# A hybrid encoder's dilated attention stage: scores over the used keys, v's parts summed in PSUM, weights split over two steps

## The chip, the cores and the metric

One of the eight cores of a Trainium2 chip runs the whole kernel. The metric is the time in microseconds (us) of one execution on the chip. Engines are named as in the profile: PE is TensorE's matmuls and PEld its weight loads, DVE is VectorE, ACT is ScalarE, POOL is GpSimd, SP is SyncE. PSUM is the accumulator memory that PE writes.

## The reference

The reference is a two-layer encoder over 1024 tokens of width 1024. Layer 0 mixes tokens with multi-head latent attention. Layer 1, which the change touches, mixes them with dilated sliding-window attention: three groups with (window, dilation) of (128, 1), (512, 4) and (2048, 16), each with its own q, k and v of 16 heads of 64, merged by their softmax denominators. Each layer ends in a squared-ReLU MLP. Of a dilated group:

```python
half = window // (2 * dilation)          # 64 in all three groups
L = S // dilation                        # 1024, 256, 64 tokens of one residue
qr, kr, vr, pr = (_to_residues(t, dilation) for t in (q, k, v, pos))
...
valid = (ki >= 0) & (ki < L) & (abs(qi - ki) <= half)
s = einsum(q, k) + bias[t5_bucket(pk - pq)]      # only where valid
```

So after tokens are put in order of their residue, a query sees at most 64 neighbours on each side, and never past its residue. In group 2 a residue has 64 tokens, and a tile of 128 tokens holds two whole residues.

## The kernel before

The program first runs in half precision: each fp32 operand is written as two fp16 parts, high and low, and a product is three matmuls (high by high, low by high, high by low). An fp32 version follows that runs only if a range check fails; in the runs here it doesn't.

`dil` (line 2191) writes the dilated stage as a list of 96 steps `("qk", g, pr, tp)` and six empty ones: group g, head pair pr (two heads), and tp, a pair of token tiles of 128 tokens. A group is 32 steps, a pair four. One turn n of the loop holds work of several steps:

- `fetch_split(n + 1)`: if step n+1 is the first of a pair, the pair's q and k weights, two raw tiles `wqkr` of 128x1024, are written as high and low parts `wqk` (`parts`: ACT line 156 for the high part, DVE line 161 for the low one). `held` ties the ACT part to the ACT instruction before it in the program.
- `attend(ready)`: for two token tiles, `products` (scores `pss`, line 2345), `scores` (bias and maximum on DVE into `pd`, exponential on ACT), the parts `ph`, and one transposing DMA on SP's queue into `pT`.
- `fetch(n)`: loads of coming weights on SP's queue; `um`: for group 2, the outputs of the groups 0 and 1 of a head pair are fetched by issues on ACT's queue.
- `project` (48 matmuls in two halves, `psproj`): q and k of a step.
- `stacks`: between the two halves, the normalized q and k (`qn`) of the step before are transposed on PE (`psq`) and copied to `kT`, the high part by ACT (line 2321) and the low one by DVE (line 2322). The next turn's `products` read both.
- `av`: probabilities times v (`psav`, lines 2424 and 2425), for the tiles scored one turn before, then the sum over v's parts into `U` (line 2432).
- `qkstep`: the norm of q and k, ending in `qn` (line 2305).

At the end of a pair in group 2, `finish` merges the groups' outputs: small factors (`mgm`, `mgf`, `mgw`, `mgd`) on DVE with one exponential on ACT, then U times mgf (line 2506) on DVE, um times mgf on POOL, and two additions U+um (line 2508) on DVE for each half. `emit` transposes the result (`psot`).

PE's instructions run in the order of the program (`pin_from`). The order of the other engines is set by a scheduler that works from the program and its dependences, so the diff doesn't tell it.

For scores, `span(g, t)` gives the columns of the 256-key window that a tile reads afterwards; before, `products` computes all 256. For group 2, `span` is 64 to 192.

Of the kernel before, what the change touches and what calls it, by code (L numbers as in the profile page):

```python
# [20 lines left out]
P = 128  # L21
# [20 lines left out]
class K:  # L42
# [1915 lines left out]
    def dil_weights(self, g, pr, alloc=None, eng=None, parts=None):  # L1958


        w_in = self.a["dil_w_in"][0]
        raws = []

        def part(half, k):
            if k == 0:
                raws.append((alloc or self.G)("wqkr", (P, 4, 256), F32))
            c0 = (g * 3 + k) * 1024 + 2 * pr * 64
            (eng or self.nc.sync).dma_start(out=raws[half][:, :, k * P : (k + 1) * P],
                                            in_=w_in[half * 512 : (half + 1) * 512, c0 : c0 + P].rearrange("(d p) f -> p d f", p=P))

        for half in range(2):
            for k in range(2):
                if parts is None:
                    part(half, k)
                else:
                    parts.append(lambda half=half, k=k: part(half, k))

        def split():
            out = []
            for raw in raws:  # L1980
                hi, lo = self.pair(self.G, "wqk", (P, 4, 256))
                self.parts(hi, lo, raw, self.ws)
                out.append((hi, lo))
            return out

        return split
# [204 lines left out]
    def dil(self, at0, at1, tail, wqk, vd, back=None):  # L2191
# [138 lines left out]
        def span(g, t):  # L2330
            if g == 2:
                return 64, 192
            n = 8 if g == 0 else 2
            return 64 if t % n == 0 else 0, 192 if t % n == n - 1 else 256

        def window(g, t):
            return t // 2 * 256 if g == 2 else min(max(P * t - 64, 0), S - 256)

        def products(u, t, pss, i):
            w0 = window(u["g"], t)  # L2340
            q = u["q"].pop(t)
            for n, (a, b) in enumerate(((0, 0), (1, 0), (0, 1))):
                for e in range(2):
                    r = slice(64 * e, 64 * e + 64)
                    nc.tensor.matmul(pss[e][:, i * 256 : (i + 1) * 256], q[r, a, :], u["k"][r, b, w0 : w0 + 256],
                                     start=n == 0, stop=n == 2)

        def bias_load(u, t=0):
# [32 lines left out]
        def attend(pairs, pe):  # L2381
# [29 lines left out]
                nc.sync.dma_start_transpose(out=flat(pT).rearrange("p (b q) -> p b q", q=P), in_=flat(ph))  # L2411
            return [(u, t, parts(pT, i)) for i, (u, t) in enumerate(pairs)]

        def av(u, t, pT):
            g, pr = u["g"], u["pr"]
            n = 1 if g == 2 else 2
            ps = PS("psav")
            for e in range(2):
                for b in range(n):
                    v = u["V"][t + b][:, (2 * pr + e) % 4, :]  # L2420
                    if self.half:
                        o = ps[:, e * 128 : (e + 1) * 128]
                        c = slice((n * e + b) * P, (n * e + b + 1) * P)
                        nc.tensor.matmul(o, pT[:, 0, c], v, start=b == 0, stop=False)
                        nc.tensor.matmul(o[:, 0:64], pT[:, 1, c], v[:, 0:64], start=False, stop=b == n - 1)
                        continue
                    o = ps[:, e * 192 : (e + 1) * 192]
                    c = slice((n * e + b) * P, (n * e + b + 1) * P)
                    nc.tensor.matmul(o, pT[:, 0, c], v, start=b == 0, stop=False)
                    nc.tensor.matmul(o[:, 0:128], pT[:, 1, c], v[:, 0:128], start=False, stop=b == n - 1)  # L2430
            k = 2 if self.half else 3
            nc.vector.tensor_reduce(u["U"][:, t, :].rearrange("p (e d) -> p e d", e=2),
                                    ps[:, 0 : 128 * k].rearrange("p (e k d) -> p e d k", e=2, k=k), op=ALU.add, axis=AX.X)
            if t == 7:
                finish(u)
            elif t == 3 and (g, pr) == (2, 7):
                last(u, 0)
# [125 lines left out]
                f()  # L2563

        def fetch_split(n):
            if n in loads:
                self.held(lambda: wts.update({firsts[n][0:3]: loads.pop(n)()}))

# [57 lines left out]
        for n, step in enumerate(steps):  # L2626
            for f in vtodo.pop(n, ()):
                f()
            turn = step is not None and step[2:] == (0, 0) and bool(perms)
            if step is not None and step[1] < 2 and step[2] == 7 and step[3] >= 2:  # L2630
                if step[3] == 2:
                    new = [[[], []], [[], []]]
                    perms = [(step[1] + 1, dp, k) for dp in range(4) for k in range(2)]
                for _ in range(step[3] - 1):
                    permute(*perms.pop(0))
            w = None
            if step is not None:
                kind, g, pr, tp = step
                w = wts[(kind, g, pr)]
                if tp == 0:  # L2640
                    units[(g, pr)] = {"g": g, "pr": pr, "q": {}, "V": VSs[(g, pr // 2)],
                                      "k": D_("kT", (P, 2, S + 512), self.DT, 2), "U": self.G("U", (P, 8, P), F32)}
                u = units[(g, pr)]
            if self.half and step is not None and tp == 0:
                bias_load(u)
            fetch_split(n + 1)
            transposed, scored = scored, attend(ready, n > end) if ready else []
            fetch(n)
            for u_, t_, _ in scored:
                if u_["g"] == 2:  # L2650
                    if u_["pr"] < 7:
                        if t_ == 7:
                            um(u_, (0, 1))
                    elif t_ in (1, 5):
                        um(u_, (t_ // 4,))
            if turn:
                h = [(lambda k, d, t=t: t[k][d // 2][:, d % 2, :]) for t in new]
                ahead = [PS("psproj") for _ in range(2)]
                both(w, ahead, (0, 1))
                ps = ahead.pop(0)  # L2660
            elif step is not None and ahead:
                ps = ahead.pop(0)
            elif step is not None:
                ps = PS("psproj")
                project(h, w, ps, 0, 2 * tp)
                one = True
            ready, carry = carry, []
            stk.append(stacking)
            if len(stk) > 1:
                x = stk.pop(0)  # L2670
                if x is not None:
                    stacks(*x)
                    u_, tp_ = x[:2]
                    if u_["g"] == 2:
                        ready = ready + [(u_, 2 * tp_), (u_, 2 * tp_ + 1)]
                    else:
                        ready = ready + ([(u_, 2 * tp_ - 1), (u_, 2 * tp_)] if tp_ else [(u_, 0)])
                        carry = [(u_, 7)] if tp_ == 3 else []
            if turn:
                both(w, [ps] + ahead, (2, 3))  # L2680
                HT = new
            elif one:
                project(h, w, ps, 1, 2 * tp + 1)
            one = False
            if step is not None:
                if step[1:3] == (2, 7):
                    tail(tp)
            late, merged[:] = late + merged, []
            while late and (step is None or late[0][1] < n):
                u_, _, ths = late.pop(0)  # L2690
                emit(u_, ths)
            for x in transposed:
                x[0]["at"] = n
                av(*x)
            stacking = None
            if step is not None:
                stacking = (u, tp, qkstep(u, tp, ps))
                if n == end:
                    self.pin_from(mark, mybir.EngineType.PE)
                    banks.close()  # L2700
                    first = banks.enter_context(tc.tile_pool(name="psY", bufs=4, space=PSUM, reuse_waits="tile"))
                    psp[0] = ctx.enter_context(tc.tile_pool(name="psT", bufs=4, space=PSUM, reuse_waits="tile"))
                    if not self.half:
                        for pp in range(3):
                            self.reload(O, src, pp, 0, nc.sync)
            if self.half and n == end + 1:
                back()
                for pp in range(3):
                    self.reload(O, src, pp, 0, nc.sync)
# [197 lines left out]
```

## Time and profile before

| | before |
|---|---|
| median of 3 runs | 3000.55 us (2996.95 to 3000.91) |
| the profiled execution | 2996.41 us, span 2994.6 us |
| mean granted clock | 0.983 |
| PE, DVE, ACT, POOL busy | 2829.0, 2252.4, 1685.8, 922.5 us |
| dilated stage in the trace | about 1548.8 to 2303.5 us |

The rows of the profile give, for an instruction, its start, its duration in us, the engine, the line in the kernel, and what it writes and reads. In brackets stands how long the engine was idle before it and what ended that. In a table of groups, "busy, mean ns | idle before" is for all instructions of that form. In the table of waits, the columns are the total, how often, and the longest. PE's matmuls overlap one another, so that a row's duration is longer than the distance to the next start; the distance is what one costs.

### The profile page before, as it was taken

How to read it: one execution, taken by the hardware profiler on the slowest of the kernel's cores; microseconds unless marked ns; L12 is line 12 of the kernel's file. 1: busy time of each engine (PE TensorE's matmuls, PEld its weight loads, DVE VectorE, ACT ScalarE, POOL GpSimd, SP SyncE). 2: the span in 40 equal slices, each digit the busy share in tenths (PEclk: the TensorE clock that was granted, in tenths of full speed). 3: DMA queues.
4: the chain of work that ended last, by engine and by line, in shares of the span. 5: the costliest groups of instructions: out<-in, count | busy, mean ns of one | idle time of the engine just before them, and what ended most of it. 6: DMA issues, size and time to landing. Idle time of an engine off the chain costs nothing. (4 is left out here: it accounts for less than half of the span.)

```text
span 2994.6 us, 54486 instructions
## 1 busy us (share of the span) xinstructions
PE 2829.0 (94%) x20148; PEld 1679.2 (56%) x20148; DVE 2252.4 (75%) x4906; ACT 1685.8 (56%) x3491; POOL 922.5 (31%) x1272
## 2 busy tenths in 40 slices
PE   6878999999999999999999989988998999999998
PEld 5634566644444444444468878877875444444443
DVE  5687777658988866788768877777886699779565
ACT  4677888825455534543227777776664365555341
POOL 6578888700211000001123334454552001110010
PEclk9999999999999999999999999999998999999999
DMA  6267464325654799546536656665766455456753
GB/s 208 69 172 157 102 116 102 125 85 184 237 198 169 248 266 300 189 170 215 181 117 145 153 124 165 148 136 126 150 130 171 139 205 203 164 185 245 241 195 86
DMA packets 589680, 503.08 MB, mean 168 GB/s; under 512 B 292277, under 2 KB 482018, under 8 KB 589402
## 3 DMA queue, kind: packets, MB, share of 16 engines
q1 hardware_dynamic: 553722, 400.74, 48.2%
q0 software_dynamic: 25248, 87.22, 7.9%
q10 hardware_dynamic: 10432, 11.54, 1.7%
q8 instruction: 159, 2.61, 0.4%
q14 instruction: 119, 0.97, 0.1%
HBM read 317.40 MB, written 125.12 MB: 148 GB/s over the span
## 5 line engine op out<-in xcount | busy, mean ns | idle before, releaser
L532 PE MATMUL psm<-hf,wf 128*128 128x512 f16 x896 | 340.3, 380 | 5.4 <-ACT wf L156 5.4
L533 PE MATMUL psm<-d,d 128*128 128x512 f16 x896 | 340.2, 380 | 4.7 <-DVE d L161 4.7
L534 PE MATMUL psm<-hf,wf 128*128 128x512 f16 x896 | 334.7, 380 | 7.9 <-DVE wf L161 7.9
L534 PE MATMUL psm<-d,d 128*128 128x512 f16 x896 | 340.2, 380 | 0.0
L533 PE MATMUL psm<-hf,wf 128*128 128x512 f16 x896 | 340.1, 380 | 0.0
L532 PE MATMUL psm<-d,d 128*128 128x512 f16 x896 | 334.7, 380 | 0.3 <-ACT d L156 0.3
L1276 POOL TENSOR_TENSOR pp<-p,pp 128x1024 f16<-128x1024 f32 x125 | 275.4, 2209 | 57.9 <-ACT pp L1269 47.2
L532 PE MATMUL psproj<-wqk,hTp 128*128 128x256 f16 x1024 | 283.3, 277 | 0.0
L533 PE MATMUL psproj<-wqk,hTp 128*128 128x256 f16 x1024 | 282.9, 276 | 0.0
L534 PE MATMUL psproj<-wqk,hTp 128*128 128x256 f16 x1024 | 282.6, 276 | 0.0
L156 ACT ACTIVATE d<-ufr 128x1024 f16<-128x1024 f32 x112 | 117.8, 1052 | 210.2 <-PE psm L534 170.8
L897 DVE TENSOR_REDUCE mx<-pmx 128x1 f32<-128x512 f32 x240 | 162.9, 688 | 78.7 <-PE pmx L895 77.4
L161 DVE SCALAR_TENSOR_TENSOR d<-ufr,d 128x1024 f16<-128x1024 f32 x112 | 136.6, 1219 | 75.6 <-ACT d L156 75.5
L1268 ACT ACTIVATE p<-pss 128x512 f32<-128x512 f32 x256 | 149.9, 590 | 43.2 <-PE pss L1259 41.7
L2372 ACT ACTIVATE pd<-pd,dnb 128x192 f32<-128x192 f32 (+2 forms) x384 | 167.3, 437 | 4.8 <-POOL y L2301 1.7
L534 PEld LDWEIGHTS <-wf 128*128 128x128 f16 x896 | 87.7, 98 | 118.5 <-DVE wf L161 13.9
L532 PEld LDWEIGHTS <-wf 128*128 128x128 f16 x896 | 87.8, 98 | 113.3 <-ACT wf L156 10.8
L534 PEld LDWEIGHTS <-d 128*128 128x128 f16 x896 | 87.8, 98 | 110.7 <-issue 5.9
L2410 POOL TENSOR_TENSOR ph<-pd,ph 128x512 f16<-128x512 f32 (+1 forms) x121 | 114.0, 948 | 113.2 <-ACT ph L2409 112.8
L533 PEld LDWEIGHTS <-d 128*128 128x128 f16 x896 | 87.8, 98 | 106.2 <-issue 2.0
L532 PEld LDWEIGHTS <-d 128*128 128x128 f16 x896 | 87.9, 98 | 106.0 <-issue 1.7
L533 PEld LDWEIGHTS <-wf 128*128 128x128 f16 x896 | 87.8, 98 | 104.3 <-issue 0.8
(440 smaller groups left out, 8136.2 us busy)
## 6 DMA issues: line engine op xcount, KB each, us to landing
ufr<-uf SPq DMA_DIRECT2D x112, 512.0 KB
w2r<-in_mlp_w SPq DMA_DIRECT2D x96, 512.0 KB
adaw<-in_ada_w SPq DMA_DIRECT2D x80, 512.0 KB
w1r<-in_mlp_w SPq DMA_DIRECT2D x64, 512.0 KB
wqkr<-in_dil_w_in SPq DMA_DIRECT2D x96, 256.0 KB
wvr<-in_dil_w_in SPq DMA_DIRECT2D x34, 512.0 KB
uf<-ub POOLq DMA_DIRECT2D x32, 512.0 KB, 3.8
uf<-ua POOLq DMA_DIRECT2D x32, 512.0 KB, 3.3
```

What stands on the lines that cost most here:

```text
L156: nc.scalar.activation(hi, src, AF.Copy, scale=scale)
L161: return nc.vector.scalar_tensor_tensor(lo, src, scale, hi, op0=ALU.mult, op1=ALU.subtract, accum_out=self.seen[:, self.nseen - 1 : self.n ...
L532: mm(out, lh, rh, start=first, stop=False)
L533: mm(out, lh, rl, start=False, stop=False)
L534: mm(out, ll, rh, start=False, stop=last)
L897: nc.vector.tensor_reduce(maxes[h][:, 2 * j + b : 2 * j + b + 1], ps, op=ALU.max, axis=AX.X)
L1268: nc.scalar.activation(p[:, b * 512 : (b + 1) * 512], ps[b], AF.Exp, scale=1.0 / self.ss)
L1276: eng.tensor_tensor(q[:, 1], p, q[:, 0], op=ALU.subtract)
L2372: nc.scalar.activation(p[:, e, lo:hi], p[:, e, lo:hi], AF.Exp, scale=1.0 / self.ss, bias=nb[:, e : e + 1], accum_out=stat[:, g, t, 1, 2 * ...
L2410: (nc.gpsimd if i or u["g"] == 2 else nc.vector).tensor_tensor(lo, p, hi, op=ALU.subtract)
```

## The change

Three edits, all in the half-precision path:

1. `products` computes scores only over the columns that `span` names: 128 of 256 in all 64 tiles of group 2, 192 in all 64 tiles of group 1, 192 in the first and last tile of a pair (16 tiles) of group 0, and 256 in the rest.
2. `avs` takes the place of `av`: the outputs of the two token tiles of a turn go into one PSUM tile, and the products with v's high and low parts are added in PSUM. For each head and block there are three matmuls of 64 columns in place of one of 128 and one of 64, and a copy of both tiles (128x256) in place of two sums over parts. In all, psav goes from 640 + 640 matmuls to 1920, and 192 reduces become 113 copies (79 of two tiles, 34 of one).
3. `fetch_split` writes the parts of the first half of a pair's weights one turn earlier, the second half where both were.

```diff
-        def split():
-            out = []
-            for raw in raws:
+        out = []
+
+        def split(n=2):
+            while len(out) < n:
                 hi, lo = self.pair(self.G, "wqk", (P, 4, 256))
-                self.parts(hi, lo, raw, self.ws)
+                self.parts(hi, lo, raws[len(out)], self.ws)
+                if n < 2:
+                    raws[len(out)] = None
                 out.append((hi, lo))
             return out
...
         def products(u, t, pss, i):
             w0 = window(u["g"], t)
+            c0, c1 = 0, 256
+            if self.half:
+                c0, c1 = (x - w0 + P * t - 64 for x in span(u["g"], t))
...
-                    nc.tensor.matmul(pss[e][:, i * 256 : (i + 1) * 256], q[r, a, :], u["k"][r, b, w0 : w0 + 256],
+                    nc.tensor.matmul(pss[e][:, i * 256 + c0 : i * 256 + c1], q[r, a, :], u["k"][r, b, w0 + c0 : w0 + c1],
                                      start=n == 0, stop=n == 2)
...
+        def avs(xs):
+            ps = PS("psav")
+            for i, (u, t, pT) in enumerate(xs):
+                pr = u["pr"]
+                n = 1 if u["g"] == 2 else 2
+                for e in range(2):
+                    o = ps[:, i * P + e * 64 : i * P + e * 64 + 64]
+                    for b in range(n):
+                        v = u["V"][t + b][:, (2 * pr + e) % 4, :]
+                        c = slice((n * e + b) * P, (n * e + b + 1) * P)
+                        nc.tensor.matmul(o, pT[:, 0, c], v[:, 0:64], start=b == 0, stop=False)
+                        nc.tensor.matmul(o, pT[:, 0, c], v[:, 64:128], start=False, stop=False)
+                        nc.tensor.matmul(o, pT[:, 1, c], v[:, 0:64], start=False, stop=b == n - 1)
+            us = [x[0] for x in xs]
+            if len(xs) == 2 and us[0] is us[1]:
+                t = xs[0][1]
+                nc.vector.tensor_copy(us[0]["U"][:, t : t + 2, :], ps[:, 0 : 2 * P].rearrange("p (i e) -> p i e", i=2))
+            else:
+                for i, (u, t, _) in enumerate(xs):
+                    nc.vector.tensor_copy(u["U"][:, t, :], ps[:, i * P : (i + 1) * P])
...
         def fetch_split(n):
+            if self.half and n + 1 in loads:
+                self.held(lambda: loads[n + 1](1))
             if n in loads:
                 self.held(lambda: wts.update({firsts[n][0:3]: loads.pop(n)()}))
...
             for x in transposed:
                 x[0]["at"] = n
-                av(*x)
+                if not self.half:
+                    av(*x)
+            if self.half and transposed:
+                avs(transposed)
```

The scheduler's order moves with it. The following places are all at the end of a head pair of group 2 (the second to the third step of the pair after it). In the program's names, ISA is the instruction that adds the bias and takes the maximum (`pd`); a first `kT` row and a second one bound the third step.

On DVE, the rows right after the first kT of a pair, before:

```order
L2322 SCALAR_TENSOR_TENSOR kT_27301<-psq_27640,kT_27301 128x2x256
L2506 TENSOR_TENSOR U_26744<-U_26744,mgf_27815 128x512
L2508 TENSOR_TENSOR U_26744<-U_26744,um_27609 128x512
L2432 TENSOR_REDUCE U_26744<-psav_27671 128x128
L2432 TENSOR_REDUCE U_26744<-psav_27677 128x128
L2296 TENSOR_REDUCE dms_27684<-dsq_27683 128x8
L2508 TENSOR_TENSOR U_26744<-U_26744,um_27609 128x512
```

and now:

```order
L2325 SCALAR_TENSOR_TENSOR kT_27726<-psq_28072,kT_27726 128x2x256
L2519 TENSOR_TENSOR mgw_28249<-mgf_28248,stat 128x48
L2437 COPY U_27161<-psav_28103 128x256
L2299 TENSOR_REDUCE dms_28118<-dsq_28117 128x8
L2520 TENSOR_REDUCE mgd_28247<-mgw_28249 128x16
```

The multiplication of U and the additions of um have left this place, and the merge's small operations, which stood ahead of the first kT, have come to it. One copy stands for two reduces.

On DVE, the rows right before the second kT, before:

```order
L134 SCALAR_TENSOR_TENSOR drt_27689<-dms_27684,dry_27687 128x8
L135 SCALAR_TENSOR_TENSOR drt_27689<-drt_27689,dry_27687 128x8
L161 SCALAR_TENSOR_TENSOR wqk_27702,seen_14494<-wqkr_27188,wqk_27702 128x1024
L136 SCALAR_TENSOR_TENSOR dry_27687<-drt_27689,dry_27687 128x8
L161 SCALAR_TENSOR_TENSOR wqk_27705,seen_14494<-wqkr_27484,wqk_27705 128x1024
L2305 TENSOR_TENSOR qn_27699<-psproj_27615,dry_27687 128x512
L2322 SCALAR_TENSOR_TENSOR kT_27301<-psq_27770,kT_27301 128x2x256
```

and now:

```order
L134 SCALAR_TENSOR_TENSOR drt_28123<-dms_28118,dry_28121 128x8
L2522 TENSOR_TENSOR mgf_28248<-mgf_28248,mgd_28247 128x48
L135 SCALAR_TENSOR_TENSOR drt_28123<-drt_28123,dry_28121 128x8
L2532 TENSOR_TENSOR U_27161<-U_27161,mgf_28248 128x512
L136 SCALAR_TENSOR_TENSOR dry_28121<-drt_28123,dry_28121 128x8
L161 SCALAR_TENSOR_TENSOR wqk_28136,seen_14494<-wqkr_27911,wqk_28136 128x1024
L2308 TENSOR_TENSOR qn_28133<-psproj_28047,dry_28121 128x512
L2534 TENSOR_TENSOR U_27161<-U_27161,um_28041 128x512
L2325 SCALAR_TENSOR_TENSOR kT_27726<-psq_28201,kT_27726 128x2x256
L2534 TENSOR_TENSOR U_27161<-U_27161,um_28041 128x512
```

One of the two splits is gone from here (it stands ahead of the first kT now), and the multiplication of U and one addition of um have come in; the second addition comes behind the kT. In the pairs in which v is split in this step too, a `vs` row stands here besides, and both additions stand ahead of the kT.

On ACT, the rows before the first kT of a pair, before:

```order
L132 ACTIVATE drl_27559<-dms_27555,misc 128x8
L133 ACTIVATE dry_27558<-drl_27559 128x8
L2370 ACTIVATE dnb_27592<-stat,ln_16275 128x2
L2370 ACTIVATE dnb_27601<-stat,ln_16275 128x2
L2372 ACTIVATE pd_27589,stat<-pd_27589,dnb_27592 128x128 x2
L2372 ACTIVATE pd_27598,stat<-pd_27598,dnb_27601 128x128 x2
L2492 ACTIVATE mgf_27815<-mgf_27815 128x48
L2409 ACTIVATE ph_27587<-pd_27589 128x256
L2409 ACTIVATE ph_27587<-pd_27598 128x256
L2321 ACTIVATE kT_27301<-psq_27640 128x2x256
```

and now:

```order
L156 ACTIVATE wqk_28002<-wqkr_27611 128x1024
L2376 ACTIVATE dnb_28024<-stat,ln_16275 128x2
L2566 DMA um_28041<-U 64x4x256
L2376 ACTIVATE dnb_28033<-stat,ln_16275 128x2
L2566 DMA um_28041<-U 64x4x256
L2378 ACTIVATE pd_28021,stat<-pd_28021,dnb_28024 128x128 x2
L2378 ACTIVATE pd_28030,stat<-pd_28030,dnb_28033 128x128 x2
L2566 DMA um_28044<-U 64x4x256
L2415 ACTIVATE ph_28019<-pd_28021 128x256
L2566 DMA um_28044<-U 64x4x256
L2415 ACTIVATE ph_28019<-pd_28030 128x256
L2324 ACTIVATE kT_27726<-psq_28072 128x2x256
```

One split and the four issues of um (which stood a step earlier) have come in ahead of the kT, and the merge's exponential `mgf` has gone behind it. In the third step ACT has one split where it had two.

In groups 0 and 1 every second pair has its two splits in two steps now; in the others both still stand in one step. PE's order is the program's.

More of the change, by code (lines that the diff above doesn't have):

```diff
@@ L2412, in attend @@
             return [(u, t, parts(pT, i)) for i, (u, t) in enumerate(pairs)]
+        def avs(xs):
[18 more added lines that the diff above has]
+                    nc.vector.tensor_copy(u["U"][:, t, :], ps[:, i * P : (i + 1) * P])
+            for u, t, _ in xs:
+                if t == 7:
+                    finish(u)
+                elif t == 3 and (u["g"], u["pr"]) == (2, 7):
+                    last(u, 0)
         def av(u, t, pT):
@@ L2420, in av @@
                     v = u["V"][t + b][:, (2 * pr + e) % 4, :]
[L2421 to L2426, printed above, removed]
                     o = ps[:, e * 192 : (e + 1) * 192]
@@ L2430, in av @@
                     nc.tensor.matmul(o[:, 0:128], pT[:, 1, c], v[:, 0:128], start=False, stop=b == n - 1)
-            k = 2 if self.half else 3
             nc.vector.tensor_reduce(u["U"][:, t, :].rearrange("p (e d) -> p e d", e=2),
-                                    ps[:, 0 : 128 * k].rearrange("p (e k d) -> p e d k", e=2, k=k), op=ALU.add, axis=AX.X)
+                                    ps[:, 0:384].rearrange("p (e k d) -> p e d k", e=2, k=3), op=ALU.add, axis=AX.X)
             if t == 7:
```

## The prediction

> **What bounds the kernel now.** I read the first page first, for who is busy and at what clock.
>
> ```profile
> span 2994.6 us, 54486 instructions
> PE 2829.0 (94%) x20148; PEld 1679.2 (56%) x20148; DVE 2252.4 (75%) x4906; ACT 1685.8 (56%) x3491; POOL 922.5 (31%) x1272
> ```
>
> PE is busy 94% of the span, so a gain has to come from work of PE or from its 165 us of idle time. Next the busy time by stretch, for the three head groups of the dilated stage (g = 0, 1, 2), which are all the change touches. The columns are the length, then PE, PEld, DVE, ACT and POOL busy, and the granted clock.
>
> ```profile
> 1548.80:1794.70 245.90, 235.77 (x2516) 202.79 (x2515) 192.61 (x620) 189.13 (x552) 94.05 (x190) 0.98 0.58 133
> 1794.70:2042.90 248.20, 235.88 (x2562) 204.44 (x2561) 187.29 (x641) 185.87 (x566) 108.73 (x245) 0.99 0.63 146
> 2042.90:2303.50 260.60, 230.11 (x2277) 193.96 (x2276) 210.63 (x689) 164.73 (x562) 123.42 (x204) 0.95 0.65 144
> ```
>
> PE leads in all three. Its idle time is largest in g = 2, 260.60 - 230.11 = 30.5 us, where DVE is busiest. What PE waited for (us in total, times, longest), over the stage:
>
> ```profile
> PE psav L2424 <- DMA pT<-ph: 17.8, 11, 4.1
> PE pss L2345 <- DVE kT L2322: 13.0, 11, 2.8
> PE pss L2345 <- ACT kT L2321: 7.4, 9, 1.7
> ```
>
> Two kinds of stall: PE ahead of psav waits for the transposed probabilities pT, and PE ahead of the scores waits for the two copies of kT. In g = 2 the second kind lies in the third step of a head pair, as this stretch of the timeline shows (start, duration; the steps around it take 6.88 us, this one 9.05):
>
> ```profile
> 2173.27 4.94 POOL L2506 TENSOR_TENSOR um<-um,mgf 128x512 f32<-128x512 f32 x4
> 2173.36 1.50 DVE L2506 TENSOR_TENSOR U<-U,mgf 128x512 f32<-128x512 f32 x1
> 2174.95 1.36 DVE L2508 TENSOR_TENSOR U<-U,um 128x512 f32<-128x512 f32 x1
> 2176.23 0.74 DVE L2432 TENSOR_REDUCE U<-psav 128x128 f32<-128x256 f32 x2
> 2177.49 1.27 DVE L2508 TENSOR_TENSOR U<-U,um 128x512 f32<-128x512 f32 x1
> 2178.05 1.99 ACT L156 ACTIVATE wqk<-wqkr 128x1024 f16<-128x1024 f32 x2
> ...
> 2179.80 1.22 DVE L161 SCALAR_TENSOR_TENSOR wqk<-wqkr,wqk 128x1024 f16<-128x1024 f32 x1
> ...
> 2181.02 1.22 DVE L161 SCALAR_TENSOR_TENSOR wqk<-wqkr,wqk 128x1024 f16<-128x1024 f32 x1
> ...
> 2182.50 0.28 PE L2345 MATMUL pss<-kT 64*128 64x256 f16 x2 [1.18 <-ACT kT L2321]
> ...
> 2182.77 0.68 DVE L2322 SCALAR_TENSOR_TENSOR kT<-psq,kT 128x512 f16<-128x512 f32 x1
> ...
> 2183.51 0.72 PE L2345 MATMUL pss<-kT 64*128 64x256 f16 x10 [0.73 <-DVE kT L2322]
> ```
>
> DVE works without a gap from 2173.36 to its kT's end at 2183.45, 10.1 us for a step in which PE has 6.9 us of work. Two splits of 1.22 us stand ahead of its kT, two of 1.0 us ahead of ACT's. I put the loss at 9.05 - 6.88 = 2.2 us in each of the six pairs that have the next pair's weights to split.
>
> **Scores.** In a steady step of g = 1 PE's starts give the prices:
>
> ```profile
> 1885.40 0.22 PE L2424 MATMUL psav<-vs,pT 128*128 128x128 f16 x1
> 1885.46 0.19 PE L2425 MATMUL psav<-vs,pT 128*128 128x64 f16 x1
> 1885.49 0.22 PE L2424 MATMUL psav<-vs,pT 128*128 128x128 f16 x1
> ...
> 1886.05 0.19 PE L2425 MATMUL psav<-vs,pT 128*128 128x64 f16 x1
> 1886.18 0.83 PE L2345 MATMUL pss<-kT 64*128 64x256 f16 x12
> 1886.94 0.28 PE L532 MATMUL psproj<-wqk,hTp 128*128 128x256 f16 x1
> ```
>
> Twelve score matmuls run as six concurrent pairs (one head in each half of the array) from 1886.18 to 1886.94; a projection of the same 256 columns starts every 0.109 us (six such are 0.65, the rest is the switch). So a pair costs 0.109 us, 0.43 ns a column. A tile has three pairs. By columns, g = 2 saves 64 x 3 x 128 x 0.43 = 10.5 us, g = 1 saves 64 x 3 x 64 x 0.43 = 5.3, g = 0 saves 16 x 3 x 64 x 0.43 = 1.3: 17.1 at most. At least it saves nothing, if a fixed cost of a pair hides the columns; the next rows make that unlikely, so I take the upper end, but only where PE is not waiting anyway: six of g = 2's 32 steps are bound by DVE, and some seven more, its first pair and its tail, by other waits, which leaves 10.5 x 19/32 = 6.2. In g = 1 and g = 0 I take 5.0 and 1.2. Together 12.4.
>
> **v's parts in PSUM.** Sixteen psav instructions now start between 1885.40 and 1886.05, so a 128-column matmul and its 64-column partner cost 0.085 us. The change puts three of 64 columns in their place. The same form (65, 64, 65 columns, each with a weight load of its own) stands in layer 0's attention:
>
> ```profile
> 265.57 0.19 PE L1291 MATMUL pav<-hv,pp 128*128 128x65 f16 x1
> ...
> 265.91 0.19 PE L1293 MATMUL pav<-hv,pp 128*128 128x65 f16 x1
> ```
>
> Eleven steps in 0.34 us: 31 ns each, 93 ns a triple. Bounds are three times the 64-column partner's 28 ns (84) and 93. For 640 triples that is -0.6 to +5.1 us; the layer-0 rows are nearest, but have 65 columns in two of three, so I take 89: +2.6. On DVE a copy of 128x256 takes the place of two reduces. Nearest rows, both reading PSUM:
>
> ```profile
> L2432 DVE TENSOR_REDUCE U<-psav 128x128 f32<-128x256 f32 x186 | 75.0, 417 | 35.1 <-PE psav L2425 34.4
> L2366 DVE CUSTOM_DVE_ANT_0 pd<-pss,bt 128x256 f32<-128x256 f32 x96 | 36.1, 418 | 0.0
> ```
>
> The two reduces took 0.74 us, one copy of 256 columns is put at 0.41, so DVE is relieved of 0.33 us a step. That is beside PE's work in all steps but those where DVE is last, and is counted there alone. The reader waits for both tiles' matmuls, 0.35 us later for the first tile; U is needed by finish or the merge, one or more steps on, so this is at nothing.
>
> **The split over two steps.** In g = 2, by the order on DVE, the third step loses one split (-1.22), has one copy for two reduces (-0.33), has its second U+um behind kT (-1.27), and takes on the small merge operations that stood in the step before, shown by these rows (mgw, mgd, reciprocal, the last mgf):
>
> ```profile
> 2171.66 0.21 DVE L2493 TENSOR_TENSOR mgw<-mgf,stat 128x48 f32<-128x48 f32 x1 [0.73 <-ACT mgf L2492]
> ...
> 2172.43 0.31 DVE L2496 TENSOR_TENSOR mgf<-mgf,mgd 128x48 f32<-128x48 f32 x1
> ```
>
> From 2171.66 to 2172.75, +1.0. So 10.1 - 1.2 - 0.3 - 1.3 + 1.0 = 8.3 us between the two kT, 1.8 less. ACT loses one split too, 1.0 us, and its exponentials start sooner since both heads of a tile now come first. So three of the six pairs gain 1.8. The other three also convert a part of v there (0.69 us, row below) and have both U+um ahead of kT: 8.3 + 1.3 + 0.7 is 10.3, no gain. The step before gets a split (1.22) and loses the merge operations (1.0): level on DVE. ACT gets the split (1.0) there and the four issues that fetch um, and loses one exponential (mgf). These rows show its cover:
>
> ```profile
> 2163.67 0.69 DVE L161 SCALAR_TENSOR_TENSOR vs<-vraw,vs 128x512 f16<-128x512 f32 x1
> ...
> 2165.93 0.58 ACTq L2540 DMA_DIRECT2D um<-U  x1
> ...
> 2166.24 0.57 ACT L2321 ACTIVATE kT<-psq 128x512 f16<-128x512 f32 x1
> ...
> 2172.15 0.57 ACT L2321 ACTIVATE kT<-psq 128x512 f16<-128x512 f32 x1
> ...
> 2174.36 0.83 PE L2345 MATMUL pss<-kT 64*128 64x256 f16 x12
> ```
>
> ACT's first kT of the pair ended at 2172.72, and PE used it at 2174.36, so 1.6 us are spare for a split of 1.0. The issue at 2165.93 didn't keep ACT's next kT from starting at 2166.24, inside its 0.58 us. So I put this at nothing; if that cover is gone, PE waits for the first kT (second rival). Gain 5.4, and about 1 at the first pair. What is late next in those steps is still DVE's kT, by some 0.4 us. In g = 0 and g = 1 the splits of every second pair change step but hide behind PE, and the other pairs keep both in one step. The waits for pT there do not move: the transposition queues behind the bulk loads of v and ends with them,
>
> ```profile
> 1982.72 4.44 SPq L2411 DMA_TRANSPOSE pT<-ph  x1
> ...
> 2173.34 1.23 SPq L2411 DMA_TRANSPOSE pT<-ph  x1
> ```
>
> 4.44 us for what takes 1.23 (for half the columns) when no bulk load runs, so a ph that is ready sooner gains nothing; PE only arrives sooner and waits longer, which costs about 1 us of the scores' gain.
>
> **Sum.** -12.4 + 2.6 - 5.4 - 1 + 1 = -15.2 us, plus or minus 5 for the two passages between groups and the tail, whose order hardly changes. The profiled execution took 2996.41 us (its span and 1.8 around it), so 2981; the median of the runs is 4.1 higher, and on that footing it is 2985.5. I give 2986.
>
> The Trainium skill's page "TensorE: Matmul & The Clock Gate", section "Back-to-back issue gap", says that sustained pairs of a weight load and a matmul cost about 81 ns each at 128 columns, set by both operations. The trace disagrees: 31 ns at 64 columns in layer 0, 85 ns for a whole psav pair. By that figure an estimate for a triple would be 243 ns, +101 us over the 640, and the sum about +80: the third rival's mechanism at a higher price, which these rows leave almost no chance.
>
> The same skill's "GPSIMD Engine Reference", section "Specifications", says that POOL shares its SBUF interfaces with VectorE and that instructions with two SBUF inputs contend. The trace agrees: U+um took 1.36 us beside POOL's um where its median is 0.69. It would make the merge ahead of kT dearer, as in the first rival.
>
> **Rivals.** *The merge keeps the stall (0.20).* U times mgf and U+um now stand in the third step after the maxima of the scores, and POOL's um runs beside them. How dear that is shows in their shortest, median and longest times:
>
> ```profile
> L2508 DVE TENSOR_TENSOR U<-U,um x28: 676/693/1527, 2090.8 to 2287.4; 128x512 f32<-128x512 f32 x28
> ```
>
> If both stay at 1.4 us or wait for um from POOL, which now starts later, the third step stays at 9 us in all pairs. Then -12.4 + 2.6 + 1 = -9, or -5 where a second step of each pair loses its gain in scores too: 2992 to 2996. For it: DVE has no gap there now. Against it: 1.8 us less to do.
>
> *A new stall one step earlier (0.08).* ACT's split and four um issues of 0.58 us stand ahead of the pair's first kT. If the issues do block ACT, that is 1.0 + 2.3 us against 1.6 spare: 1.7 us late in seven pairs, +12, 2998. For it: the order. Against it: the kT at 2166.24.
>
> *The weight loads set PE's pace (0.07), the other side.* PE's loads go from two to three for each head and block. If the present 0.085 us are two loads of 42 ns, a triple takes 127: 640 x 42 = +27 us; and a score pair can't fall below two loads of 42, so scores give only 64 x 3 x 0.025 x 2 = 9.6. With the split's 6 the sum is +11: 3012. It decides from about 106 ns a triple on (640 x 21 = 13.4, against 15.4 gained). Against it: psav's starts alternate 0.06 and 0.03 us, as the columns do, and layer 0's 31 ns.
>
> **How the numbers follow.** Forecast 0.65, rivals 0.20, 0.08 and 0.07. Medians of this kernel tell apart about 0.2%, 6 us. Faster by more: the forecast but for 0.01, and half of the first rival, 0.74. Slower: the third rival and a little of the second, 0.09. The rest, 0.17, is the same. The range holds the forecast with its bounds (all stalls of g = 2 gone, 13 us instead of 6, and the passages 5 better: 2973) and reaches over the first two rivals to 3001, leaving out the third and the edges.
>
> **What would show it.** In the profile after: score pairs of 128 columns in about 55 ns; triples of psav at 84 to 93 ns; PE busy in g = 2 lower by about 10 us, in g = 1 by 4; one copy of about 0.4 us in place of two reduces; the third step of a pair in g = 2 at 7 to 7.5 us in every second pair, and 9 in the others; waits for pT unchanged. Wrong if the wait for kT turns up in the second step, if triples take over 100 ns, or if the passages between groups move by over 5 us.

## The result: 16 us less, and the profile after

| | before | after |
|---|---|---|
| median | 2999.51 us (5 runs) | 2983.52 us (5 runs, 2982.67 to 2985.34) |
| ratio after/before | | 0.9949, 95% interval 0.9934 to 0.9963 |
| profiled execution | 2996.41 us, span 2994.6 | 2985.34 us, span 2983.5 |

The change makes the kernel 0.51% faster; 2986 had been forecast. The profiled execution of after took as long as the slowest of its five runs, and that of before less than any of its five, so the two traces differ by only 11 us. A second profile of after (below) has a span of 2979.3 us. Both are used where the sum matters. The medians and ratios below leave out single executions that ran far slower than the others of their kernel.

The first page after, span and busy times:

```profile
span 2983.5 us, 55654 instructions
PE 2818.9 (94%) x20788; PEld 1680.0 (56%) x20788; DVE 2233.1 (75%) x4827; ACT 1687.5 (57%) x3491; POOL 925.9 (31%) x1272
```

Busy time by head group after (length, PE, PEld, DVE, ACT, POOL, granted clock), cut at the same events as before:

```profile
1550.70:1789.10 238.40, 230.17 (x2752) 201.50 (x2750) 183.46 (x588) 184.71 (x539) 87.25 (x185) 1.00 0.61 140
1789.10:2036.60 247.50, 233.83 (x2819) 205.17 (x2818) 182.34 (x617) 188.69 (x574) 101.76 (x242) 0.97 0.64 146
2036.60:2294.50 257.90, 224.39 (x2415) 192.65 (x2414) 205.97 (x670) 166.99 (x565) 139.84 (x210) 0.94 0.68 146
```

PE has 5.6, 2.1 and 5.7 us less to do, DVE 9.2, 5.0 and 4.7. PE's idle time in group 2 is 257.90 - 224.39 = 33.5 us, 3 more than before, and the granted clock there is 0.94 where it was 0.95. POOL is busy 16 us longer there, with nearly the same instructions.

What PE waited for in the stage after (us in total, times, longest):

```profile
PE psav L2431 <- DMA pT<-ph: 19.3, 12, 2.8
PE pss L2351 <- DVE kT L2325: 17.4, 14, 3.6
PE pss L2351 <- DVE qn L2308: 7.0, 1, 7.0
PE psot L2551 <- DVE U L2534: 4.0, 2, 3.8
PE pss L2351 <- ACT kT L2324: 2.2, 2, 1.5
```

ACT's kT is hardly waited for now (7.4 before), but DVE's more (13.0 before). The waits of the table have not become fewer in sum.

PE's starts in a step without a wait, first in group 1, then the scores of one in group 2:

```profile
1824.28 0.19 PE L2431 MATMUL psav<-vs,pT 128*128 128x64 f16 x1
1824.31 0.19 PE L2432 MATMUL psav<-vs,pT 128*128 128x64 f16 x1
1824.34 0.19 PE L2433 MATMUL psav<-vs,pT 128*128 128x64 f16 x1
...
1824.95 0.19 PE L2433 MATMUL psav<-vs,pT 128*128 128x64 f16 x1
1825.08 0.67 PE L2351 MATMUL pss<-kT 64*128 64x192 f16 x12
...
2129.31 0.51 PE L2351 MATMUL pss<-kT 64*128 64x128 f16 x12
```

From 1824.28 to 1824.95 stand 23 distances of 29 ns, so a triple costs 87 ns (forecast 89, before 85). The row of twelve scores is 0.83 us long for 256 columns, 0.67 for 192 and 0.51 for 128, 0.16 less for each 64 columns. The copies of two tiles took what was put for them (minimum, median, longest ns):

```profile
L2437 DVE COPY U<-psav x78: 361/415/425, 1574.9 to 2308.0; 128x256 f32<-128x256 f32 x78
```

Where the time went is told by the length of each step, from one group of psq transposes to the next. In us, after less before, for the two profiles of after:

| part | first | second |
|---|---|---|
| steps without a wait (groups 0, 1, 2: -0.8, -2.9, -3.1) | -6.8 | -6.9 |
| steps that wait for pT in groups 0 and 1 | +2.4 | -0.7 |
| third steps of group 2, two pairs without a part of v | -3.4 | -3.4 |
| third steps of group 2, two pairs with a part of v | +5.4 | +5.4 |
| first and last of the merging pairs of group 2 | +0.7 | +0.3 |
| the two passages between groups | -5.7 | -6.7 |
| the tail of the stage | -3.4 | -3.5 |
| ahead of and behind the stage | -0.3 | +0.2 |
| sum | -11.1 | -15.3 |

**The third step split in two.** Here is one that got longer, after (psq to psq: 2139.31 to 2151.12, 11.8 us where it was 9.1). POOL's four products are shown first as one row, then the first three apart:

```profile
2138.83 6.40 POOL L2532 TENSOR_TENSOR um<-um,mgf 128x512 f32<-128x512 f32 x4 [2.49 <-DVE mgf L2522]
...
2138.83 1.37 POOL L2532 TENSOR_TENSOR um<-um,mgf 128x512 f32<-128x512 f32 x1 [2.49 <-DVE mgf L2522]
2140.16 1.57 POOL L2532 TENSOR_TENSOR um<-um,mgf 128x512 f32<-128x512 f32 x1
2141.68 2.10 POOL L2532 TENSOR_TENSOR um<-um,mgf 128x512 f32<-128x512 f32 x1
...
2139.22 1.00 DVE L135 SCALAR_TENSOR_TENSOR drt<-drt,dry 128x8 f32<-128x8 f32 x1
2140.14 0.68 DVE L2532 TENSOR_TENSOR U<-U,mgf 128x512 f32<-128x512 f32 x1
2140.74 1.00 DVE L136 SCALAR_TENSOR_TENSOR dry<-drt,dry 128x8 f32<-128x8 f32 x1
2141.67 1.21 DVE L161 SCALAR_TENSOR_TENSOR wqk<-wqkr,wqk 128x1024 f16<-128x1024 f32 x1
...
2142.81 1.52 DVE L2534 TENSOR_TENSOR U<-U,um 128x512 f32<-128x512 f32 x1
...
2144.85 0.93 DVE L2534 TENSOR_TENSOR U<-U,um 128x512 f32<-128x512 f32 x1
2145.70 0.68 DVE L2325 SCALAR_TENSOR_TENSOR kT<-psq,kT 128x512 f16<-128x512 f32 x1
...
2146.44 0.45 PE L2351 MATMUL pss<-kT 64*128 64x128 f16 x10 [3.40 <-DVE kT L2325]
```

An operation on 128x8 numbers takes 1.00 us, and ends at 2140.22, when POOL's product ends (2138.83 + 1.37 = 2140.20). The next, `dry`, ends at 2141.74, again with POOL's (2140.16 + 1.57 = 2141.73). Then DVE's split starts, and POOL's third product, from 2141.68, takes 2.10 us, the split's time and its own. So the two engines take turns, each waiting for a whole instruction of the other, and DVE's rows of 1.00, 1.00 and 1.52 us hold such a wait. The Trainium skill's page "SBUF — State Buffer", section "Who interferes with whom", states that a DVE instruction with two SBUF inputs contends with a POOL instruction that reads SBUF, and that the shared ports are an exclusive lock; that the lock is held for the whole instruction it says of DVE's 2-port modes. The trace agrees, and shows whole instructions here too: 1.00 us, where the same line takes 0.16 in the kernel without POOL's products (below).

PE's wait of 3.40 us is only a part of the 11.8. Behind it PE's projections start 0.21 us apart, where they start 0.11 apart at first:

```profile
2146.82 0.28 PE L532 MATMUL psproj<-wqk,hTp 128*128 128x256 f16 x1
2146.94 0.27 PE L533 MATMUL psproj<-wqk,hTp 128*128 128x256 f16 x1
...
2147.22 0.42 PE L532 MATMUL psproj<-wqk,hTp 128*128 128x256 f16 x1
2147.43 0.42 PE L533 MATMUL psproj<-wqk,hTp 128*128 128x256 f16 x1
```

The same table as by head group, for the step before the wait and for a stretch behind it, shows why: the granted clock (third number from the end) was 1.00 and is 0.50.

```profile
2132.40:2139.30 6.90, 6.72 (x78) 5.88 (x77) 5.65 (x23) 5.74 (x21) 4.10 (x7) 1.00 1.21 191
2147.10:2150.50 3.40, 3.40 (x19) 2.34 (x17) 3.40 (x15) 2.65 (x11) 1.49 (x4) 0.50 0.34 77
```

So the step is 6.7 us of work, 3.4 of waiting, and 1.7 lost in 3.4 us at half the clock, in both of these pairs and in both profiles; before, these steps held no such stretch. In all traces kept here, PE's waits of 3 us or more in the stage up to 2250 us all have such a stretch behind or beside them, and shorter ones, of 2.1 to 2.5 us, only some. A step that waits a little longer can so become 1.7 us longer, or not, and this bears on several experiments below.

In two of the pairs without a part of v only one small operation meets POOL ahead of kT, and PE waits little:

```profile
2171.77 1.01 DVE L136 SCALAR_TENSOR_TENSOR dry<-drt,dry 128x8 f32<-128x8 f32 x1
...
2176.02 0.45 PE L2351 MATMUL pss<-kT 64*128 64x128 f16 x10 [0.58 <-DVE kT L2325]
```

That step takes 7.3 us, where it took 9.0.

The last of the merging pairs has no part of v either, but its step went only from 9.0 to 8.6 us, and the step before it from 6.9 to 8.0 (7.7 in the second profile). There the wait of the prediction's second rival came, in the second step of the pair. An issue that fetches um stood in ACT's queue for 2.13 us, from 2225.69 to 2227.82; ACT's next instruction began at 2227.92, and the first kT was late:

```profile
2225.69 2.13 ACTq L2566 DMA_DIRECT2D um<-U  x1
...
2227.92 0.40 ACT L2378 ACTIVATE pd<-pd,dnb 128x128 f32<-128x128 f32 x1 [1.47 <-POOL most L2305]
...
2230.71 0.23 PE L2351 MATMUL pss<-kT 64*128 64x128 f16 x2 [0.66 <-ACT kT L2324]
2231.44 0.45 PE L2351 MATMUL pss<-kT 64*128 64x128 f16 x10 [0.50 <-DVE kT L2325]
```

The merge came later by as much, and `drt` and `dry` both took 1.0 us here without any part of v. Why this issue took 2.13 us, where others take 0.58, the trace does not show.

### The profile page after: what moved, and what is told of

It reads as the page before. It is cut to its first block, busy times and chain, and to the rows that moved or that the text cites. A ratio compares the mean times of both kernels' runs of the same rounds, so it can differ in the third digit from the quotient of the medians.

```text
span 2983.5 us, 55654 instructions
## 1 busy us (share of the span) xinstructions
PE 2818.9 (94%) x20788; PEld 1680.0 (56%) x20788; DVE 2233.1 (75%) x4827; ACT 1687.5 (57%) x3491; POOL 925.9 (31%) x1272
```

## The experiments

### One edit at a time

Each kernel is the one before with one of the three edits as in the diff above.

```diff
# scores_only: products alone
+            if self.half:
+                c0, c1 = (x - w0 + P * t - 64 for x in span(u["g"], t))
...
```

> The kernel before with the narrow scores alone (first edit). By the prediction: 0.31 us less in every step of group 2 that is not waiting, 0.15 in group 1, third step of a pair in group 2 still 9.0 us, in all 10 to 12 us less. Rival (weight loads set the pace of narrow pairs): half of that or less, steps of group 2 shorter by under 0.16 us.

Measured: 0.9988 (0.9979 to 0.9998), about 3.5 us less, where 10 to 12 had been forecast. Steps that don't wait are 0.32 us shorter in group 2 and 0.16 in group 1, just the price by columns, so the weight loads do not set the pace. But the steps that wait took it back: those that wait for pT in groups 0 and 1 are 6.5 us longer in sum, and three of the third steps of group 2 take 10.4 to 10.6 us. The waits alone did not grow by as much: PE waits 2.1 to 2.3 us in these three third steps, where it waited 1.9 to 2.0, and the rest, 1.5 to 1.7 us in each, is a stretch at half the clock behind the wait. Of the 6.5 us, 3.1 are the same. Two waits of PE in this kernel:

```profile
PE pss L2348 <- DVE kT L2322: 24.0, 14, 4.5
PE psav L2427 <- DMA pT<-ph: 19.1, 15, 2.9
```

```diff
# avs_only: av replaced by avs
-                av(*x)
...
+            if self.half and transposed:
+                avs(transposed)
```

> The kernel before with v's parts summed in PSUM and two tiles read at once, alone (second edit). By the prediction: 0.03 us more in a step with two blocks a tile, 0.02 in group 2, the third step of a pair in group 2 about 0.3 us shorter than 9.0; in all +0 to +4 us. Rival (relief of DVE is what makes the change fast): 4 us less or better, with the third steps at 8 us or below.

Measured: 0.998 (0.9971 to 0.9989), about 6 us less, where 0 to 4 more had been forecast. Steps that don't wait are 0.02 us longer in groups 0 and 1 and 0.01 in group 2, as the triples' price says. The gain stands in what waits on DVE: third steps of 8.2 to 8.3 us in three pairs (9.0 before; one rose from 9.1 to 10.5, by 1.7 us at half the clock), the passage from group 1 to 2 3.7 us less and the tail 2.4 less. This favours the rival's cause. The profiled execution is one of the slower ones of its kernel, and its span is only 0.7 us below that of before.

```diff
# split_only: weights' parts in two turns
...
+            if self.half and n + 1 in loads:
+                self.held(lambda: loads[n + 1](1))
```

> The kernel before with the weights' split over two steps alone (third edit). By the prediction: third step of a pair in group 2 at 7.3 to 8 us in every second pair, near 9 in the others; in all 4 to 6 us less. Rival (the merge beside POOL's um takes it back): 7.5 us in every second pair and over 11 in the others, in all between 2 us less and 2 us more.

Measured: 1.0024 (1.0015 to 1.0033), 7 us more: alone the edit makes the kernel slower, beyond what the rival had allowed. Third steps are 8.8 us in two pairs without a part of v (9.0 before), 11.8 in the last one, and 13.0 and 12.8 in the pairs with one (9.1 before). PE's longest wait in one of these:

```profile
2154.93 1.25 PE L2348 MATMUL pss<-kT 64*128 64x256 f16 x10 [4.32 <-DVE kT L2325]
```

These ten matmuls take 1.25 us, where they took 0.72 in the kernel before: PE runs at half the clock here too. The merge stands ahead of kT as in the changed kernel, and DVE's v part took 1.53 us and three more instructions 1.0 to 1.5, beside POOL. Why the pairs without a part of v gained only 0.2 us alone, and 1.7 with the other edits, was not tried.

### The change without the third edit

```diff
# no_split: the changed kernel, less
...
-            if self.half and n + 1 in loads:
-                self.held(lambda: loads[n + 1](1))
```

> The changed kernel without the third edit (weights split in one step as before). If the third edit is worth 5 us as predicted: 5 us slower than the changed kernel, about 10 us faster than before, third steps of all pairs in group 2 at 8.5 to 9 us. If the merge beside POOL's um takes its gain back in every second pair: within 2 us of the changed kernel.

Measured: 0.9963 (0.995 to 0.9976), 11 us less than before. That is near the sum of the first two edits alone (3.5 + 6). Third steps are 8.4 us in the pairs without a part of v, 10.6 and 8.9 in the others. These two differ by the clock: PE waits 2.3 and 2.1 us in them, and only the first has a stretch at half the clock behind it. The two kernels were run again together:

> The changed kernel again, beside the next one on the same chip: 15 to 16 us faster than before, third steps of group 2's pairs at 7.3 and 11.8 us in turn, as in its first profile.

> The changed kernel without the third edit, again, beside the changed one. If the third edit's gain in one half of the pairs is lost in the other: within 3 us of the changed kernel. If it is worth what was predicted: 5 us slower.

Measured: the change 0.9957 (0.9944 to 0.9971), median 2981.46; without the split 0.9967 (0.9954 to 0.9981), median 2987.01. The ratios' intervals overlap in both comparisons, so what the third edit is worth beside the other two, between nothing and some 6 us, stays open. What the traces do show is its two sides: third steps of 7.3 against 8.4 us, and of 11.8 twice against 10.6 and 9 (in the repeat 9.1 and 10.6).

### Is it POOL, or v's part?

```diff
# no_um_product: the changed kernel, in merge, for the first seven pairs
+                if self.half and k < 2 and u["pr"] < 7:
+                    nc.vector.scalar_tensor_tensor(U, y, 2.0 ** -30, U, op0=ALU.mult, op1=ALU.add)
+                    continue
```

> The changed kernel without POOL's product of um with its factors in the merge of the first seven pairs of group 2; the two additions on DVE stand where they were. If POOL's um beside DVE makes the third step long in every second pair (11.8 us): that step falls to 9.5 us or less, the 128x8 operations there take 0.2 us where they took 1.0, U+um 0.7. If it is the amount of DVE's own work (v's part, split and merge in one step): it stays over 11 us.

This kernel leaves out the products with the merge's factors; the additions on DVE are kept, with a constant in the factors' place. The step of 11.8 us fell to 7.7. The same rows in it:

```profile
2131.34 0.16 DVE L135 SCALAR_TENSOR_TENSOR drt<-drt,dry 128x8 f32<-128x8 f32 x1
...
2132.02 0.16 DVE L136 SCALAR_TENSOR_TENSOR dry<-drt,dry 128x8 f32<-128x8 f32 x1
...
2133.24 0.69 DVE L2532 SCALAR_TENSOR_TENSOR U<-um,U 128x512 f32<-128x512 f32 x1
...
2136.16 0.45 PE L2351 MATMUL pss<-kT 64*128 64x128 f16 x10 [0.99 <-DVE kT L2325]
```

0.16, 0.16 and 0.69 us, where POOL's products made them 1.00, 1.00 and 1.52: 2.5 us. PE's wait fell by 2.4 us with them, and the 1.7 us at half the clock are gone as well, which makes the 4.1 us of the step. One run took 2967.25 us beside a median of 2997.46 before, 30 us less, where the change gains 13 to 16. So by this one run POOL's 28 products cost this kernel about as much as the whole change gains. What part of that is DVE's longer rows, and what part the wait for the products themselves (in the first pair PE had waited 3.8 us for U, and that step fell from 14.6 to 9.0 us), was not tried.

```diff
# vs_skip: the changed kernel with
+                    skip = 1 if self.half and g == 2 and pr and t else 0
-                    vtodo.setdefault(n - 2 + late + t // 2, []) ...
+                    vtodo.setdefault(n - 2 + late + skip + t // 2, []) ...
```

> The changed kernel with v's parts in group 2 made in four turns that leave out the one with the merge and the second half of the split. If the collision of the three makes the step of 11.8 us: 7.3 us in all pairs, 7 to 10 us less than the changed kernel in all. If POOL's um alone makes it: 10 us or more in every second pair, no gain.

Measured: 0.9935 (0.9921 to 0.9948), median 2978.69. The two long third steps are 7.29 us now, as in the other pairs, though POOL's products still run and `dry` still takes 1.00:

```profile
2137.00 1.00 DVE L136 SCALAR_TENSOR_TENSOR dry<-drt,dry 128x8 f32<-128x8 f32 x1
...
2141.25 0.45 PE L2351 MATMUL pss<-kT 64*128 64x128 f16 x10 [0.54 <-DVE kT L2325]
```

So either alone removes the long step in these two pairs: it takes POOL's products and v's part together. The part of v delays `drt` and `dry` into POOL's products and brings both additions ahead of kT. In time the gain on the changed kernel is 3 to 6 us, by medians and ratios whose intervals still overlap, about half of the 9 that the two steps gave, since the steps after them and the pair at the end gave some back.

```diff
# skip_no_split: vs_skip, less
...
-            if self.half and n + 1 in loads:
-                self.held(lambda: loads[n + 1](1))
```

> The changed kernel without the third edit, and with v's parts in group 2 moved out of the merge's turn. If the third edit only pays once v's part is out of the way: third steps of 8.4 us in all pairs where the one with v's parts moved has 7.3, and 4 to 6 us slower than that one. If moving v's parts is all that counts: the same time as that one.

Measured: 0.9964 (0.995 to 0.9978), median 2985.29. Its interval does not meet that of the kernel above, and its third steps are 8.25, 8.25, 8.24 and 7.94 us in the four pairs where that one has 7.3. So once v's part is out of the way the third edit is worth about 1 us in each of these, 3.5 us together, and 6 to 9 us in all by the medians and ratios, from runs on two chips. Where the rest stands is not shown: the profiled execution here, 2976.47, was the fastest of its five by far, and below that of the kernel above; the step lengths are from it.

### What is left

```diff
# early_split: vs_skip with
+            m = n + 1 if self.half else n
...
-                self.held(lambda: loads[n + 1](1))
...
+                self.held(lambda: loads[m + 1](1))
```

> As the one with v's parts moved, and both halves of the weights' split one turn earlier (with their loads), so that no split stands in the merge's step. If DVE's queue ahead of kT is what is left there: third steps at 6.6 to 6.9 us, 10 to 13 us less than the changed kernel. If ACT or POOL is next: third steps stay at 7.3 us, and it equals the one with v's parts moved.

The weights' loads are issued one turn earlier too. Measured: 0.9951 (0.9937 to 0.9964), no faster than the change. Of six third steps three are at 6.6 us as forecast; but the step before takes 8.4 to 10.2 us in four pairs, and 13.7 in the first, where it took 6.9. Some rows of one:

```profile
2133.51 0.58 ACTq L2566 DMA_DIRECT2D um<-U  x1
2134.14 0.60 ACT L2324 ACTIVATE kT<-psq 128x512 f16<-128x512 f32 x1 [1.52 <-PE psav L2433]
...
2134.79 0.23 PE L2351 MATMUL pss<-kT 64*128 64x128 f16 x2 [1.19 <-ACT kT L2324]
```

ACT sat idle for 1.52 us until the last issue that fetches um was out at 2134.09, and its kT came right behind, though psq had been written since 2130.6. (The mark at kT names PE's psav, which ended just as the issue began.) By the trace's semaphores the issue waited for the semaphore on which a load of wqkr, issued on SP's queue at 2129.12, landed until 2133.49, and it began 0.02 us later. This is the second rival of the prediction: an issue on ACT's queue holds what stands behind it while it waits itself. Three other issues in this step, with nothing left to wait for, held nothing.

```diff
# staged_v: early_split with one of three loads a turn
-                vtodo.setdefault(n - 4, []).append(VS["load"])
+                for j in range(3 if g < 2 else 2):
+                    vtodo.setdefault(n - 4 + j * (1 if self.half else 0), []).append(... v_load(g, c, VS["raws"], j))
```

> As the one with early splits, and v's bulk loads issued in three turns in place of one. If pT is late because its transposition stands behind the whole bulk of v: the waits of psav for pT (19 us in the stage) fall below 9 us, 8 to 12 us less again. If the loads and the transposition share the memory's bandwidth wherever they are issued: the waits move to the next steps and the time stays within 3 us.

Measured: 0.9929 (0.9915 to 0.9943), median 2976.76. The waits for pT in groups 0 and 1 are gone from the steps in which v is loaded (7.24 and 7.08 us, as in steps without a wait), 5.1 us less than before there; in the stage they fall to 12.6 us, not below 9, since the other half lies in group 2 and the passages, with the stalls of the early splits.

```diff
# staged_skip: vs_skip with the staged loads, splits as in the changed kernel
-                vtodo.setdefault(n - 4, []).append(VS["load"])
...
+                    vtodo.setdefault(n - 4 + j * (1 if self.half else 0), []).append(... v_load(g, c, VS["raws"], j))
```

> The changed kernel with v's parts in group 2 moved and v's bulk loads issued in three turns; the split as in the changed kernel. The waits for pT in groups 0 and 1 vanish as they did with early splits, and the new stalls of the early splits in group 2's first steps do not come: 2968 to 2973 us. If the stalls at the passages between groups grow by as much: no faster than the one with v's parts moved.

Measured: 0.9914 (0.99 to 0.9927), median 2969.72, 26.5 us less than before, the fastest here but for the one without POOL's products. A transposition beside v's loads, in the changed kernel and in this one, and PE's wait for pT in this one:

```profile
1862.07 5.22 SPq L2417 DMA_TRANSPOSE pT<-ph  x1
```

```profile
1862.93 2.83 SPq L2424 DMA_TRANSPOSE pT<-ph  x1
```

```profile
PE psav L2438 <- DMA pT<-ph: 11.3, 9, 3.3
```

That step went from 11.2 us (9.0 in the second profile, without a stretch at half the clock) to 7.13. So pT was late for standing behind v's whole bulk, and not for the bandwidth alone.

## Why the prediction was right, and where only its sum was

The time, 2983.5, lies within 3 us of the forecast, and the change gained 16.0 us where 15.2 were worked out. That the sum came out so near is in part luck: its terms miss by up to 10 us and cancel. Two of the prediction's own signs of being wrong came true: the passages between the groups moved by over 5 us (-5.7 and -6.7), and in one pair the wait for kT turned up in the second step. By its terms:

- **The prices on PE were right.** Scores: 0.33 us a step in group 2 and 0.16 in group 1 by its columns, 0.32 and 0.16 measured alone. The triple: 89 ns forecast, 87 measured. The copy: 0.41 us forecast, 0.415 measured. The third rival (weight loads set the pace) is out. PE's busy time, though, fell by 5.7 us in group 2 and 2.1 in group 1 where 10 and 4 had been forecast. The difference is the clock: less what the stretches at half the clock add to it (half of PE's busy time in them), it fell by 9.4 and 4.8.
- **How much of it reached the end was counted in the wrong places.** -12.4 + 2.6 = -9.8 us had been counted, and the steps without a wait gave -6.8. The steps that wait for pT passed nothing on, and the price of arriving early was put at 1 us where narrow scores alone lost 6.5 in the waits for pT, 3.1 of them by the clock. Over the whole stage it adds up otherwise. PE's work, reckoned at the full clock, fell by 14.7 us in both profiles, as all columns and triples of the prediction make it (-17.1 + 2.6 = -14.5). PE's idle time and its loss at half the clock were together 69.4 us before and 73.2 and 68.5 after. So the gain is PE's own work, and the stalls were moved rather than removed.
- **The split's term had the wrong sign.** -5.4 and -1 were forecast, and the third steps and the first and last pair gave +2.7 and +2.3 in sum. In two pairs without a part of v the third step was forecast at 1.8 us less and gave 1.7, but not as worked out: DVE's time between the two kT fell from 10.0 to 7.4 us, not to 8.3, and the first kT came 0.8 to 0.9 us later after its psq, though the step before had been called level. In the pairs with a part of v, 10.3 us were forecast between the two kT, and they took 10.1 (2136.24 to 2146.38). The step that failed is the comparison: 10.3 was set against the 10.1 of a pair without a part of v and called no gain, while these pairs had taken 9.2 before (2143.41 to 2152.64). PE's wait grew from 2.0 to 3.4 us, and the half clock behind it, for which the prediction has no term, added 1.7; 2.7 us were lost in each. The first rival, which priced U times mgf and U+um beside POOL, named the mechanism behind DVE's long time, but not that the smallest instructions (`drt`, `dry`: 1.00 us) pay as much.
- **The new wait on ACT came in one step only:** PE waited 0.66 us for ACT's first kT in the last pair, and 2.2 us in all, where the second rival had put 1.7 us in each of seven pairs. The row from which it was argued that an issue holds nothing was read too freely, as this pair and the kernel with early splits show.
- **The waits for pT** were forecast unchanged, and were, in sum: 17.8 before, 19.3 and 16.9 after.
- **The passages and the tail** were put at 0, plus or minus 5, because their order hardly changes. They gave 9 to 10 us, and that is what made the sum come out. By the traces 3.5 us of it is PE's own work at the full clock, 4.3 and 3.2 are less time at half the clock, and 1.3 and 3.5 less idle time. With v's parts summed alone the passages gave 2.9 and the tail 2.4; with narrow scores alone 1.4 and 1.4. Which instruction ends the waits there was not tried, and single profiles differ by 1 to 2 us at these places, so why the idle time and the half clock shrank stays open.

## What to carry to other kernels

A price read from the distance between starts holds to a few ns; what fails is counting it in steps that wait for something else, so count only the steps whose end that engine sets, and ask of the others what they will wait for longer. Read the granted clock behind a long wait of PE: here a wait of 3.4 us cost 5.1. Where a scheduler moves DVE work with two SBUF inputs beside POOL work, price every such instruction, however small, at POOL's remaining time, not at its own duration. And before work is moved to the step before, look at what already stands there: moving v's part by one turn and issuing v's loads in three turns together gained another 11 to 14 us on the change.

## What the runs showed of the hardware

- A 128x8 DVE operation of 0.16 us took 1.00 beside POOL's 128x512 products and ended within 0.02 us of one of them; POOL's product in turn took 2.10 us behind a split of 1.21. POOL's products had run 1.04 to 1.56 us each in the trace before.
- After PE had waited 3.40 us its granted clock was 0.50 for 3.4 us: projections started 0.21 us apart in place of 0.11, and 1.7 us were lost.
- An issue in ACT's queue that waited for the landing of another DMA held the activation behind it (1.52 us idle), and one that lasted 2.13 us, for a reason that is not shown, did so too (1.47 us idle). Three issues of 0.58 to 0.83 us with nothing left to wait for did not.
- Three 64-column matmuls, each with its own weight load, cost 29 ns each, so a third weight load in place of 64 more columns was nearly free (87 against 85 ns).
- A transposing DMA that stood behind v's bulk lasted 5.22 us on SP's queue, and 2.83 with that bulk cut in three.
